# A hybrid encoder block on one core: the last pair's products ahead of the gate in front, the channel matrix in halves, a single-column first factor, and source order to the end

## The chip, the cores and the metric

The kernel runs on one core of one Trainium2 chip. A core has TensorE (matrix products into PSUM), VectorE, ScalarE and GpSimd (called PE, DVE, ACT and POOL in the profile) and SyncE (SP), whose queue issues most of the DMAs here. The metric is the device time of one execution in microseconds; lower is better.

## The reference

One layer of an encoder is applied to two sequences of 2048 tokens with 1024 features, with shared weights. Per sequence, all in float32:

```python
u = rmsnorm(h, g_norm)
q, k, v, ga, f, gf = split(u @ w_in)            # 512, 128, 128, 512, 512, 512 columns
q, k = rope(rmsnorm(q, g_q)), rope(rmsnorm(k, g_k))   # 8 q heads, 2 kv heads of 64; 2-D axial positions
a  = softmax(q k^T / 8) v * silu(ga)            # bidirectional
fo = (real(fft2(f over positions, 64 channels)) @ w_fmix per group) * silu(gf)
h  = h + concat(a, fo) @ w_out
h  = h + (p @ w_ple) * sigmoid(rmsnorm(h, g_ple) @ w_ple_gate)
y  = rmsnorm(h, g_final)
```

## The kernel before

Products that need float32 accuracy are made from float16 parts: an operand is split into a high part (`h`) and a low part (`l`), and a product is three matmuls, high by high, high by low and low by high (`SPLIT3`). A transposed operand is made by a transposing DMA. The kernel has two phases.

**Phase 1, `project`.** Tokens are taken in 16 pairs of 128-token tiles (8 pairs per sequence), in the loop `iteration(i)`, i up to 19, with `n` = 16. A pair passes through a software pipeline: load and normalise (`hi_u`, `lo_u`), q and kv products (`mm_tile(i, 0)` and `mm_tile(i, 1)`, in tiles `wr_q`, `wr_kv`), squares and Newton steps for q's and k's norms (`square_z`, `newton`, L669 to L687), norm and rotary position (`norm_q`, `rope_q`, with POOL's adds on L773), high and low parts (`hi_q` on ScalarE, L785; `lo_q` on VectorE, L797 to L801), and the transposes of q and k on SyncE's queue (L805, L808), whose results are stored one iteration later (L806, L810; in the last iteration by POOL's queue).

The remaining products of a pair are its sweep: a generator (`sweep_chunk`) that makes the f columns (8 steps), the gf columns (16), the first Fourier factor (1), and the gate ga (32 steps of three 256-column matmuls). Each `next` emits one step and returns its nominal time; `sweep_part(us)` takes steps up to a budget. So the budgets written in `iteration` decide where a pair's f, gf and gate products stand among the others. In iteration i the sweep is that of pair i-1. After a gate's matmuls, ScalarE takes the tanh (L1114), VectorE makes the SiLU from PSUM (L1117) and its maximum (L1095). Every fourth step also takes one step of `self.ahead`, which makes the maxima of the first attention units' scores (L1363, L1371) and then issues the transposition of the first unit's row maxima (`max_rows`, tile `mr`, L1387); every fifth takes one of `bg`, which prepares the far weights.

**Phase 2, attention with a filling.** `attention` runs 64 units (2 sequences, 2 kv heads, 16 query tiles) of 8 steps: scores (L1333, the first of them with `mr`), exponentials (ScalarE, L1336), row sums (POOL, L1341), maxima two units ahead (L1363, L1371), products with v (L1399). `interleave` fills the rest of TensorE with the generator `fill`: first `fourier2` (second factor of the position DFT, L1243, then the channel matrix `bd`, L1189, which is loaded from DRAM by L1220), then `outp`. `outp` handles 32 tiles of 128 tokens; for tile t it emits two slots `out1(t, 0..1)` (output projection and residual, L1586), then `out3(t-1, 0)`, `middle(t)`, `out3(t-1, 1)`. `middle(t)` takes squares (L1686), the norms by Newton steps (`norm`, L1692 to L1695), and makes the normalised and transposed `hT` that `out3(t, .)` needs one turn later (`out2`: L1715, L1716, L1719, L1721). `out3` ends with a tanh (L1599) and then the product with the embedding rows (`products`, on L505, sums on L1608 and L1610). A slot is 24 matmuls of 512 columns; before tile 30 the two halves of the rows of two neighbouring slots run side by side (`halves`, L1665, with the copy `seen` between), from tile 30 on (`WHOLE`) a slot is made whole (L505 in tiles `ps_x` or `ps_g`). VectorE's last operations of a slot are put off through `defer` and run at a `flush` while attention lasts (`self.dq` is a list), and at once when it has ended (`self.dq is None`).

The order on PE, ACT, DVE and SP is the order of the source in phase 1 (POOL as well) and during attention (`manual_schedule`). What is left when attention has ended is emitted by `self.drain(f)` in `run`, outside of that block, where a planner orders the instructions of all engines by its own costs. PSUM there: five banks `psD` (`ps_x`) besides the two of `psG` and one of `psF`.

Of the kernel before, what the change touches and what calls it, by code (L numbers as in the profile page):

```python
# [10 lines left out]
F32 = mybir.dt.float32  # L11
F16 = mybir.dt.float16
I32 = mybir.dt.int32
AF = mybir.ActivationFunctionType
ALU = mybir.AluOpType
# [4 lines left out]
DM = 1024  # L20
NT = 16
HD = 64
EPS = 1e-6
U_SC = 2.0 ** 8
# [21 lines left out]
_E = mybir.EngineType  # L46
# [119 lines left out]
class Build:  # L166
# [97 lines left out]
    def rsqrt(self, x, n, u="", e=None, st=None):  # L264

        st = st or self.st
        e = e or self.nc.vector
        tl = lambda m: st.tile([128, n], F32, name=f"rs{u}{n}_{m}", tag=f"rs{u}{n}_{m}", bufs=2)
        y, hx = tl("y"), tl("hx")
        e.tensor_scalar(out=y[:].bitcast(I32), in0=x.bitcast(I32), scalar1=-0.5, scalar2=float(0x5F3759DF),  # L270
                        op0=ALU.mult, op1=ALU.add)
        e.tensor_scalar(out=hx[:], in0=x, scalar1=-0.5, scalar2=None, op0=ALU.mult)
        for it in range(3):
            t, z = tl("t"), tl(f"z{it}")
            e.tensor_tensor(out=t[:], in0=y[:], in1=y[:], op=ALU.mult)
            e.tensor_tensor(out=t[:], in0=t[:], in1=hx[:], op=ALU.mult)
            c = 1.5 if it < 2 else 0.5
            w = z if it < 2 else tl("w")
            if e is self.nc.vector:
                e.scalar_tensor_tensor(out=w[:], in0=t[:], scalar=c, in1=y[:], op0=ALU.add, op1=ALU.mult)  # L280
            else:
                e.tensor_scalar(out=t[:], in0=t[:], scalar1=c, scalar2=None, op0=ALU.add)
                e.tensor_tensor(out=w[:], in0=t[:], in1=y[:], op=ALU.mult)
            if it == 2:
                e.tensor_tensor(out=z[:], in0=y[:], in1=w[:], op=ALU.add)
            y = z
        return y

    def pow2(self, name, m, exp):
# [331 lines left out]
    def project(self, P, PU, W, early, later, wkv, wq, wf, wgf, wga, bg, mid):  # L621
# [3 lines left out]
        nc, st = self.nc, self.st  # L625
# [183 lines left out]
                                        ks[:].rearrange("p v y t d -> p (v y t d)"))  # L809
            stores_next.append(lambda: self.last_stores.dma_start(self.kTd[s][:, :, c].rearrange("v p y r -> p v y r"), kT[:]))  # L810

        def sweep_part(us):

            while us > 0 and sweeps:
                try:
                    us -= next(sweeps[0])
                    if done:
                        done.append(True)
                        if len(done) % NBF == 0:
                            next(bg, None)  # L820
                        if len(done) % (NBF - 1) == 2:
                            next(self.ahead, None)
                except StopIteration:
                    del sweeps[0]
# [44 lines left out]
        def iteration(i):  # L869
# [11 lines left out]
                f()  # L881
            del stores[:]
            sq = square_z(i - 1) if ok(i - 1) else None
            if i == n + 1:
                sweep_part(3.9)
            if ok(i - 3):
                lo_q(i - 3)
            if ok(i - 2):
                rope_q(i - 2)
            rs = None  # L890
            if i == n:
                sweep_part(7.2)
            if ok(i - 1) or ok(i + 2):
                rs = newton(i - 1 if ok(i - 1) else None, i + 2 if ok(i + 2) else None, sq)
            if ok(i):
# [7 lines left out]
            if folds(i):  # L903
                fold_u(i, 0)
                fold_s(i, 0)
                fold_u(i, 1)
                sweep_part(12.0)
                fold_hl(i, 0)
                fold_s(i, 1)
            sweep_part(1000.0 if i < n else (3.3, 3.3, 7.0, 100.0)[i - n])  # L910
            if folds(i):
                fold_hl(i, 1)
            if ok(i + 2):
                hi_u(i + 2)
# [3 lines left out]
                load_x(i + 4, 1)  # L918
            if ok(i - 2):
                hi_q(i - 2)  # L920
            if ok(i):
                mm_tile(i, 1)
                append(i)
# [208 lines left out]
    def fourier2(self, pool, hook):  # L1132
# [84 lines left out]
            step()  # L1217
            yield 0.86

        nc.sync.dma_start(self.bd[:], self.bdd)  # L1220
        self.cx = pool.tile([128, 2, 128], F32, name="c2x", bufs=1)
        nc.sync.dma_start(self.cx[:], self.a["c_dft2x"].rearrange("v p c -> p v c"))
        for t in range(FP):
# [308 lines left out]
    def outp(self, pool0, ow, open_pool):  # L1532
# [87 lines left out]
        def slot(up, whole):  # L1620


            low = held.pop() if held else None
            def seen():
                j = st.tile([128, 1], F32, name="seen")
                nc.vector.tensor_copy(j[:], low[0][:, 0:1])  # L1626
# [9 lines left out]
            if up is not None:  # L1636
                ps = self.group_bank()
                for i, us in enumerate(self.mm(ps[:], up[0], up[1])):
                    yield us
                    yield from embed(i >= 6)  # L1640
                if low is not None:
                    seen()
                yield from self.after(ticket)
                yield from end(up[2](ps))
# [43 lines left out]
        def norm(ss, t):  # L1688

            ms = st.tile([128, 2], F32, name="h_ms")  # L1690
            e = nc.vector if self.dq is None or t == 0 or self.step >= 16 * N2 else nc.gpsimd
            e.tensor_scalar(out=ms[:], in0=ss[:], scalar1=1.0 / DM, scalar2=EPS, op0=ALU.mult, op1=ALU.add)  # L1692
            r = self.rsqrt(ms[:], 2, "h", e)
            q = st.tile([128, 1], F32, name="h_r")
            e.tensor_scalar(out=q[:], in0=r[:, 0:1], scalar1=U_SC, scalar2=None, op0=ALU.mult)  # L1695
            return q, r
# [68 lines left out]
        def middle(t):  # L1765

            q = r = None
            ss = st.tile([128, 2], F32, name="h_ss")
            if not (ok(t) and ok(t - 2)):
                nc.gpsimd.memset(ss[:], 1.0)  # L1770
            if ok(t - 2):
                yield from embed(True)
# [93 lines left out]
    def run(self):  # L1866
# [134 lines left out]
        self.step = 10 ** 9  # L2001
        att_stack.close()
        with pool("psD", 5, space=PSUM) as self.psX:
            self.drain(f)
        fill_stack.close()
        w_stack.close()

# [52 lines left out]
```

## Time and profile before

| | |
|---|---|
| median of 3 runs | 2585.57 us (2585.44 to 2585.97) |
| the profiled execution, own time | 2585.38 us |
| its span, first to last instruction | 2583.6 us |
| mean granted TensorE clock | 0.994 |
| TensorE busy in the span | 97% |
| phase 1 ends, first score of attention | 737.76 us |
| attention's last row sums | 2492.08 us |
| last matmul begins its group | 2572.43 us |

The first block of the page gives each engine's busy time and its share of the span. In a list of waits, a row says which instruction's group waited, for whom, how long in total, how often, and the longest. In a timeline, a row is a run of like instructions: start in us, length in us, engine, line, operation, out<-in, partitions x elements, count, and in brackets the idle time before it with what ended it. In a row of stretches, "DVE busy" and the like stand in the order PE, PEld, DVE, ACT, POOL, then the granted clock as a share of full speed. Times are from the start of the span.

### The profile page before, as it was taken

What the parts mean: (1) busy time and instruction counts of PE and PEld (TensorE: products, weight loads), DVE (VectorE), ACT (ScalarE), POOL (GpSimd) and SP (SyncE); (2) the same over time, 40 slices, a digit from 0 to 9 for tenths busy, and PEclk for the clock granted to TensorE, in tenths of its full rate; (3) what the DMA queues carried; (4) which work ended last, traced back from release to release, by engine and by line L of the source; (5) the groups of instructions that cost most, each with busy time, mean ns of one, the idle gap of its engine ahead of it and who ended that gap; (6) DMA issues with size and microseconds to landing.
All of it is one profiled execution on the core that took longest, in us unless ns stands there. A gap on an engine that the chain in (4) does not pass through costs nothing. (4 is left out here: it accounts for less than half of the span.)

```text
span 2583.6 us, 49739 instructions
## 1 busy us (share of the span) xinstructions
PE 2503.1 (97%) x19896; PEld 1381.7 (53%) x19896; DVE 1655.9 (64%) x2382; ACT 1185.5 (46%) x1983; POOL 1834.5 (71%) x1534
## 2 busy tenths in 40 slices
PE   6999999999989999999999999999999999999988
PEld 3566666666656554545555554445444554545533
DVE  7876675776566765676666666665666666666534
ACT  4443444443245545454544555445544444445532
POOL 0365453455469988888798888887887988888850
PEclk9999999999999999999999999999999999999999
DMA  8377687777287732232223233422233322322232
GB/s 260 90 202 198 187 245 209 184 195 192 62 254 226 211 90 64 56 80 73 70 56 80 60 92 77 97 66 72 64 80 79 71 74 60 71 78 77 78 76 53
DMA packets 459032, 297.91 MB, mean 115 GB/s; under 512 B 293840, under 2 KB 402128, under 8 KB 458800
## 3 DMA queue, kind: packets, MB, share of 16 engines
q1 hardware_dynamic: 437952, 256.28, 38.9%
q10 hardware_dynamic: 15712, 20.59, 2.4%
q0 software_dynamic: 5136, 17.87, 1.9%
q8 instruction: 155, 2.54, 0.4%
q14 instruction: 77, 0.63, 0.1%
HBM read 146.12 MB, written 82.45 MB: 88 GB/s over the span
## 5 line engine op out<-in xcount | busy, mean ns | idle before, releaser
L1341 POOL TENSOR_TENSOR acc<-acc,p 128x1024 f32<-128x1024 f32 x384 | 930.0, 2422 | 110.9 <-ACT p L1336 86.1
L1336 ACT ACTIVATE p<-ps_s,s_scale 128x512 f32<-128x512 f32 x1024 | 648.1, 684 | 638.2 <-PE ps_s L1333 621.9
L1371 DVE TENSOR_REDUCE a_mx<-ps_m 128x1 f32<-128x1024 f32 x498 | 608.8, 1223 | 512.7 <-PE ps_m L1363 501.5
L1665 PE MATMUL ps_g<-w_pg,hT 64*128 64x512 f16 x2784 | 494.7, 377 | 3.9 <-DVE seen L1626 2.4
L1399 PE MATMUL ps_o<-p,v 128*64 128x256 f32 x4096 | 468.1, 381 | 0.0
L1333 PE MATMUL ps_s<-q,k 64*128 64x512 f16 x3072 | 432.0, 377 | 1.4 <-ACT p L1336 1.0
L1399 PEld LDWEIGHTS ps_o<-p,v 128*64 128x64 f32 x4096 | 283.6, 137 | 159.9 <-issue 28.0
L505 PEld LDWEIGHTS <-uc 128*128 128x128 f16 x2400 | 236.1, 99 | 227.6 <-DMA uc<-hl 20.4
L1665 PEld LDWEIGHTS <-hT 64*128 64x128 f16 x2784 | 204.8, 94 | 156.6 <-issue 16.0
L1665 PE MATMUL ps_g<-w_wo,mh 64*128 64x512 f16 x1440 | 260.5, 376 | 3.8 <-DVE mh L1570 2.3
L1665 PE MATMUL ps_g<-w_wo,mT 64*128 64x512 f16 x1440 | 257.4, 376 | 0.6 <-DMA mT<-mh 0.6
L1333 PEld LDWEIGHTS <-k 64*128 64x128 f16 x3072 | 152.4, 94 | 194.9 <-issue 76.3
L1363 PE MATMUL ps_m<-k,q 64*128 64x512 f16 x996 | 200.7, 377 | 15.5 <-DVE a_mx L1371 15.3
L773 POOL TENSOR_TENSOR t<-t,t 128x640 f32<-128x640 f32 x32 | 49.3, 1560 | 205.2 <-DVE t L768 205.2
L505 PEld LDWEIGHTS <-w_ga 128*128 128x128 f16 x1536 | 148.8, 98 | 33.2 <-issue 10.4
L1339 POOL TENSOR_TENSOR acc<-p,p 128x1024 f32<-128x1024 f32 x64 | 151.0, 2359 | 13.0 <-ACT p L1336 12.2
L1665 PEld LDWEIGHTS <-mh 64*128 64x128 f16 x1440 | 101.6, 94 | 92.4 <-issue 16.8
L1665 PEld LDWEIGHTS <-mT 64*128 64x128 f16 x1440 | 107.1, 94 | 77.7 <-issue 4.8
L1422 DVE RECIPROCAL ps_f<-ps_f 128x256 f32<-128x256 f32 x61 | 107.1, 1756 | 13.6 <-PE ps_f L1415 13.6
L505 PE MATMUL ps_x<-uc,w_ga 128*128 128x256 f16 x1008 | 113.5, 273 | 0.6 <-DVE w_mxs L397 0.6
L840 POOL TENSOR_TENSOR f_s<-f_t 128x512 f32<-128x512 f32 x56 | 71.8, 1303 | 53.9 <-DVE uf L848 41.5
L1406 ACT ACTIVATE at<-ps_o,a_scale 128x256 f32<-128x256 f32 x64 | 30.4, 474 | 170.4 <-PE ps_o L1399 170.4
(343 smaller groups left out, 3363.6 us busy)
## 6 DMA issues: line engine op xcount, KB each, us to landing
q<-qTd SPq DMA_DIRECT2D x256, 64.0 KB, 2.2
ag<-agd SPq DMA_DIRECT2D x64, 256.0 KB, 3.5
out<-h POOLq DMA_DIRECT2D x31, 512.0 KB, 3.0
x<-in_x_prompt SPq DMA_DIRECT2D x16, 512.0 KB, 4.5
gfd<-gt ACTq DMA_DIRECT2D x32, 256.0 KB, 2.9
w_st<-in_w_out SPq DMA_DIRECT2D x32, 256.0 KB, 4.4
w_st<-in_w_ple_gate SPq DMA_DIRECT2D x32, 256.0 KB, 4.2
x<-in_x_sample SPq DMA_DIRECT2D x16, 512.0 KB, 5.8
```

Of the source, the lines that this page charges most:

```text
L505: self.nc.tensor.matmul(ps, lhs(ia, k), rhs(ib, k), start=(i == 0), stop=(i == 3 * ks - 1))
L773: nc.gpsimd.tensor_tensor(out=t1[:, tt], in0=t1[:, tt], in1=t2[:, tt], op=ALU.add)
L840: nc.gpsimd.tensor_tensor(out=FS[h][:, y], in0=x[:, 0], in1=x[:, 1], op=op)
L1333: nc.tensor.matmul(S[u][e][:], w[sl], q[sl].rearrange("p h q -> p (h q)"), start=j == i == 0, stop=i + 1 == len(todo), skip_group_check=True)
L1336: nc.scalar.activation(p[:, e, :], S[u][e][:], AF.Exp, scale=self.sc["s_scale"][:])
L1339: nc.gpsimd.tensor_tensor(out=ACC[u][:], in0=P[u, 0][:], in1=p[:], op=ALU.add)
L1341: nc.gpsimd.tensor_tensor(out=ACC[u][:], in0=ACC[u][:], in1=p[:], op=ALU.add)
L1363: nc.tensor.matmul(ps[c], Q[u][0][sl, h, :], kt[s, kv, half][sl, :, 0, :], start=True, stop=True)
L1371: nc.vector.reduce_max(MX[u][:, h, half, c:c + 1], x, axis=AX.X)
L1399: nc.tensor.matmul(o[64 * f:64 * f + 64], vt[s, kv, c // 8][:, c % 8, :], p[:, e, f], start=(c == 0), stop=(c == 15))
L1422: nc.vector.reciprocal(r, r)
L1665: nc.tensor.matmul(g[0][:], g[1](ia, k)[sl], g[2](ib, k)[sl], start=a, stop=z, skip_group_check=True)
```

## The change

- In the last iterations of `project` the budgets of `sweep_part` move. In iteration n-1 = 15 the rest of pair 14's gate steps is no longer swept before the second tile's q and kv products of pair 15, but in iteration 16 behind them, with `bare=True`, which takes no steps of `ahead` and `bg`. The two calls ahead of `lo_q` and ahead of `newton` go; `fold_hl(15, 1)` moves behind `hi_q(13)`. The later budgets are 13.2, 5.0 and the rest.
- `fourier2` loads the channel matrix `bd` with two DMAs, the half used first ahead of the other.
- `norm(ss, 0)`, of the first tile, uses a new `column_rsqrt`: one column, 10 instructions on VectorE with pointer scalars. The memset of `ss` on POOL is left out for tile 0.
- A whole slot in `outp` waits until attention has ended, and takes the embedding product from its fourth step on.
- The `drain` behind attention stands in a `manual_schedule` for PE, ACT, DVE and SP.

```diff
--- before.py
+++ after.py
@@ -284,6 +284,29 @@
             if it == 2:
                 e.tensor_tensor(out=z[:], in0=y[:], in1=w[:], op=ALU.add)
             y = z
+        return y
+
+    def column_rsqrt(self, ss):
+
+        st, v = self.st, self.nc.vector
+        n = 0
+
+        def op(x, a, b, o0, o1):
+            nonlocal n
+            n += 1
+            r = st.tile([128, 1], F32, name=f"cr{n}", tag=f"cr{n}", bufs=1)
+            v.tensor_scalar(out=r[:], in0=x, scalar1=a, scalar2=b, op0=o0, op1=o1)
+            return r[:]
+
+        x = op(ss, 1.0 / DM, EPS, ALU.mult, ALU.add)
+        y = st.tile([128, 1], F32, name="cr0", tag="cr0", bufs=1)[:]
+        v.tensor_scalar(out=y.bitcast(I32), in0=x.bitcast(I32), scalar1=-0.5, scalar2=float(0x5F3759DF),
+                        op0=ALU.mult, op1=ALU.add)
+        hx = op(x, -0.5, None, ALU.mult, ALU.bypass)
+        for it in range(3):
+            t = op(y, y, hx, ALU.mult, ALU.mult)
+            w = op(t, 1.5 if it < 2 else 0.5, y, ALU.add, ALU.mult)
+            y = w if it < 2 else op(w, y, U_SC, ALU.add, ALU.mult)
         return y
 
     def pow2(self, name, m, exp):
@@ -809,12 +832,12 @@
                                         ks[:].rearrange("p v y t d -> p (v y t d)"))
             stores_next.append(lambda: self.last_stores.dma_start(self.kTd[s][:, :, c].rearrange("v p y r -> p v y r"), kT[:]))
 
-        def sweep_part(us):
+        def sweep_part(us, bare=False):
 
             while us > 0 and sweeps:
                 try:
                     us -= next(sweeps[0])
-                    if done:
+                    if done and not bare:
                         done.append(True)
                         if len(done) % NBF == 0:
                             next(bg, None)
@@ -881,15 +904,11 @@
                 f()
             del stores[:]
             sq = square_z(i - 1) if ok(i - 1) else None
-            if i == n + 1:
-                sweep_part(3.9)
             if ok(i - 3):
                 lo_q(i - 3)
             if ok(i - 2):
                 rope_q(i - 2)
             rs = None
-            if i == n:
-                sweep_part(7.2)
             if ok(i - 1) or ok(i + 2):
                 rs = newton(i - 1 if ok(i - 1) else None, i + 2 if ok(i + 2) else None, sq)
             if ok(i):
@@ -904,11 +923,14 @@
                 fold_u(i, 0)
                 fold_s(i, 0)
                 fold_u(i, 1)
-                sweep_part(12.0)
+                sweep_part(12.0 if i < n - 1 else 8.6)
                 fold_hl(i, 0)
                 fold_s(i, 1)
-            sweep_part(1000.0 if i < n else (3.3, 3.3, 7.0, 100.0)[i - n])
-            if folds(i):
+            if i == n:
+                sweep_part(10.3, True)
+            elif i != n - 1:
+                sweep_part(1000.0 if i < n else (13.2, 5.0, 100.0)[i - n - 1])
+            if folds(i) and i < n - 1:
                 fold_hl(i, 1)
             if ok(i + 2):
                 hi_u(i + 2)
@@ -918,6 +940,8 @@
                 load_x(i + 4, 1)
             if ok(i - 2):
                 hi_q(i - 2)
+            if i == n - 1:
+                fold_hl(i, 1)
             if ok(i):
                 mm_tile(i, 1)
                 append(i)
@@ -1217,7 +1241,8 @@
             step()
             yield 0.86
 
-        nc.sync.dma_start(self.bd[:], self.bdd)
+        for v in (1, 0):
+            nc.sync.dma_start(self.bd[:, v], self.bdd[:, v])
         self.cx = pool.tile([128, 2, 128], F32, name="c2x", bufs=1)
         nc.sync.dma_start(self.cx[:], self.a["c_dft2x"].rearrange("v p c -> p v c"))
         for t in range(FP):
@@ -1621,6 +1646,9 @@
 
 
             low = held.pop() if held else None
+            while whole and self.dq is not None:
+                yield None
+
             def seen():
                 j = st.tile([128, 1], F32, name="seen")
                 nc.vector.tensor_copy(j[:], low[0][:, 0:1])
@@ -1637,7 +1665,8 @@
                 ps = self.group_bank()
                 for i, us in enumerate(self.mm(ps[:], up[0], up[1])):
                     yield us
-                    yield from embed(i >= 6)
+                    if i > 2:
+                        yield from embed(True)
                 if low is not None:
                     seen()
                 yield from self.after(ticket)
@@ -1688,7 +1717,9 @@
         def norm(ss, t):
 
             ms = st.tile([128, 2], F32, name="h_ms")
-            e = nc.vector if self.dq is None or t == 0 or self.step >= 16 * N2 else nc.gpsimd
+            if t == 0:
+                return self.column_rsqrt(ss[:, 0:1]), None
+            e = nc.vector if self.dq is None or self.step >= 16 * N2 else nc.gpsimd
             e.tensor_scalar(out=ms[:], in0=ss[:], scalar1=1.0 / DM, scalar2=EPS, op0=ALU.mult, op1=ALU.add)
             r = self.rsqrt(ms[:], 2, "h", e)
             q = st.tile([128, 1], F32, name="h_r")
@@ -1766,7 +1797,7 @@
 
             q = r = None
             ss = st.tile([128, 2], F32, name="h_ss")
-            if not (ok(t) and ok(t - 2)):
+            if t and not (ok(t) and ok(t - 2)):
                 nc.gpsimd.memset(ss[:], 1.0)
             if ok(t - 2):
                 yield from embed(True)
@@ -2001,7 +2032,8 @@
         self.step = 10 ** 9
         att_stack.close()
         with pool("psD", 5, space=PSUM) as self.psX:
-            self.drain(f)
+            with tc.manual_schedule(engines={_E.PE, _E.Activation, _E.DVE, _E.SP}):
+                self.drain(f)
         fill_stack.close()
         w_stack.close()
```

## The prediction

> **What bounds the kernel now.** I read the page first (busy shares, the chain that ended last), then TensorE's busy time and granted clock in stretches of 10 us, then what TensorE waited for in the stretches where it was not full, and last the order of instructions there.
>
> ```profile
> PE 2503.1 (97%) x19896; PEld 1381.7 (53%) x19896; DVE 1655.9 (64%) x2382; ACT 1185.5 (46%) x1983; POOL 1834.5 (71%) x1534
> ...
> 740.00:750.00 10.00, 3.02 (x24) 2.17 (x24) 5.99 (x11) 3.42 (x7) 3.21 (x6) 0.88 0.84 192
> 750.00:760.00 10.00, 8.77 (x48) 6.62 (x49) 3.60 (x4) 4.72 (x10) 5.46 (x7) 0.78 0.92 310
> ...
> 940.00:950.00 10.00, 6.66 (x44) 3.38 (x41) 6.47 (x6) 3.57 (x5) 9.58 (x6) 0.83 0.38 81
> ...
> PE ps_g L1189 <- DMA bd<-bdd: 5.8, 1, 5.8
> PE ps_g L1243 <- DVE gat L1117: 3.4, 1, 3.4
> ...
> PE ps_g L505 <- DVE h L1586: 4.2, 1, 4.2
> PE ps_g L1665 <- DVE seen L1626: 2.4, 1, 2.4
> ```
>
> TensorE is busy 97% of the span, so every edit counts only for the time in which TensorE stands still or runs slow. The second group of rows (length, then busy time of PE, PEld, DVE, ACT and POOL, granted clock, DMA share, GB/s) shows where: at 740 to 760, where the projections hand over to attention, and at 942 to 950, where the first tile is normalised for the gate. The last two groups are the waits of TensorE from 735 to 755 and from 2489 to 2575. The change touches just these three places.
>
> **The change part by part.** *First place: the handover at 738.* The rows are of TensorE, then VectorE and SyncE's queue, then POOL and ScalarE.
>
> ```profile
> 690.31 2.46 PE L505 MATMUL ps_x<-uc,w_ga 128*128 128x256 f16 x21
> 702.50 5.34 PE L505 MATMUL ps_g<-wr_q,uc 128*128 128x512 f16 x24
> 737.76 0.39 PE L1333 MATMUL ps_s<-mr,kone 64*128 64x512 f16 x2
> 742.39 0.94 PE L1243 MATMUL ps_g<-c,g_in 128*128 128x128 f32 x6 [3.37 <-DVE gat L1117]
> 751.23 2.05 PE L1189 MATMUL ps_g<-bd,fT 128*128 128x256 f32 x4 [5.82 <-DMA bd<-bdd]
> 753.07 1.06 PE L1243 MATMUL ps_f<-c,g_in 128*128 128x128 f32 x4
> 792.62 1.13 PE L1189 MATMUL ps_g<-bd,fT 128*128 128x256 f32 x4
> 793.59 0.61 PE L1243 MATMUL ps_f<-c,g_in 128*128 128x128 f32 x4
> ...
> 718.19 1.47 DVE L669 TENSOR_REDUCE q_ss<-sq 128x20 f32<-128x1280 f32 x1
> 723.44 0.22 DVE L687 TENSOR_SCALAR q_rs<-rsq_z,inv_kv 128x4 f32<-128x4 f32 x1
> 740.01 1.22 DVE L801 TENSOR_TENSOR qs<-t,qs 128x1024 f16<-128x1024 f32 x1
> 742.71 0.41 DVE L1117 SCALAR_TENSOR_TENSOR gat<-gat,ps_g 128x256 f32<-128x256 f32 x1
> ...
> 719.83 1.26 SPq L1387 DMA_TRANSPOSE mr<-nm  x1
> 741.29 2.61 SPq L805 DMA_TRANSPOSE qT<-qs  x2
> 744.00 2.00 SPq L808 DMA_TRANSPOSE kT<-ks  x1
> 746.06 0.97 SPq L1220 DMA_DIRECT2D bd<-bdd  x1
> ...
> mr<-nm SPq DMA_TRANSPOSE x1, 2.4
> ...
> 733.64 3.04 POOL L773 TENSOR_TENSOR t<-t,t 128x640 f32<-128x640 f32 x2 [3.96 <-DVE t L768]
> 736.71 1.06 ACT L785 ACTIVATE qs<-t 128x1024 f16<-128x1024 f32 x1 [6.22 <-POOL t L773]
> ```
>
> Both waits have one cause. The last pair's q and kv products (702.50) come after the whole gate of the pair in front (from 690.31). What follows them (square sums, Newton steps, rotary, split) reaches the low part of q only at 740.01. The last gate's SiLU (742.71) stands behind that on VectorE, and its PSUM bank is what the first Fourier product waits for: 3.4 us. On SyncE's queue the two q transposes and the k transpose (741.29, 744.00) stand ahead of the channel matrix's load (746.06), which lands at 751.2: 5.8 us.
>
> In the changed source, the sweep of the pair in front stops in iteration 15 after 8 steps of f, 16 of gf, the first factor and 5 of 32 steps of the gate; q and kv follow. So they start at 690.31 + 5 steps of 0.33 (a step is 3 matmuls; 21 took 2.46 with the last one's tail) = 692, not 702.5: 10.4 us earlier. The gate's other 27 steps go behind them; the sum of TensorE's work is the same. The chain, from the end of kv at 700: about 5 us for the older pairs' low parts and rotary on VectorE, 5.5 for the Newton steps (718.19 to 723.7), 3.4 for four gate SiLUs with their maxima, 0.41 each (742.71), that now queue behind them, 5 again for low part and rotary, 3.0 for POOL's adds (733.64), 1.9 for ScalarE (1.06 and two smaller copies), 2.8 for the low part: 727, not 741.2. VectorE is then free when the last gate leaves TensorE at 737.8, and the 3.4 us go.
>
> SyncE's queue: the transposes start at 727 to 729 (two buffers, whose stores must have landed) and take 2.6 + 2.0 us (741.29, 744.00). Behind them now stands the transposition of the first unit's maxima (mr, 719.83 before): the stretch marked bare takes no step of the maxima, so eight steps slip and mr is issued after the last pair's transposes. That is the added wait: issue at 732 to 734, landing 2.4 later (the row of transfers) or, with others in front, up to 3.5: 734 to 737.5, and the first score matmul (737.76) needs it. Late mr costs TensorE one for one; the cover is 0 to 3.5 us. The channel matrix's first half is issued right behind, at 733 to 735; the whole took 5.2 from issue to use, so the half is there by 740, and its first use falls at 742. The 5.8 us go. The second half costs one more issue on a queue that nobody waits for there; without that cover it is half of the 0.97 row. The bank of the postponed gates is held until VectorE comes to them, near 714; the products that take those banks next come at 712 to 720, so I book some loss.
>
> The clock: after the waits the same forms took 2.05 for 1.13 and 1.06 for 0.61 (751.23 and 753.07 against 792.62 and 793.59): with the next group about 1.6 us lost, which go too. The Trainium skill (TensorE: Matmul & The Clock Gate, Part 1: The HAM clock gate) has the clock halve after an idle window of about 3.4 us and stay so for a window; by it the price would be an estimated 1.7 us for each wait at 742 and 751, 3.4 in all. Against it, the dip at 940 to 950 (0.83) stands at a wait of 2.2 us, shorter than that window, so I take the rows.
>
> Bounds of this place: at best 3.4 + 5.8 + 1.6 = 10.8; at worst the 3.4 alone. For late mr and held banks I take 1.0 off: **9.8 gained**.
>
> *Second place: the first tile's factor.*
>
> ```profile
> 937.62 0.28 DVE L1692 TENSOR_SCALAR h_ms<-h_ss 128x2 f32<-128x2 f32 x1
> 940.10 0.15 DVE L1695 TENSOR_SCALAR h_r<-rsh_z 128x1 f32<-128x1 f32 x1
> 945.96 0.61 PE L1363 MATMUL ps_m<-k,q 64*128 64x512 f16 x2 [2.24 <-DVE a_mx L1371]
> ```
>
> 14 small instructions from 937.62 to 940.25, 0.19 each, become 10. The removed POOL memset stood in nobody's way. Two-column tensors become columns with operands by pointer, whose price no small row here shows; L687 with a pointer scalar took 0.22 (723.44), L1695 with a constant 0.15, so 7 of them may give back 0.5. Gain 0.3 to 0.8; TensorE's wait at 945.96 ends with this chain. **0.5.**
>
> *Third place: the end.* Two edits: the last two tiles' products wait until attention has ended (and so take the five new banks, not the two that the halves use), and four engines keep source order.
>
> ```profile
> 2495.76 0.39 PE L505 MATMUL ps_x<-w_wo,mh 128*128 128x512 f16 x1
> 2512.09 2.58 PE L505 MATMUL ps_g<-wp,pT 128*128 128x512 f16 x6 [4.18 <-DVE h L1586]
> 2547.82 5.34 PE L505 MATMUL ps_x<-w_pg,hT 128*128 128x512 f16 x24
> 2553.01 1.46 PE L505 MATMUL ps_g<-wp,pT 128*128 128x512 f16 x6
> 2554.30 5.34 PE L505 MATMUL ps_x<-w_pg,hT 128*128 128x512 f16 x24
> 2572.43 1.46 PE L505 MATMUL ps_g<-wp,pT 128*128 128x512 f16 x6
> ...
> 2548.81 1.06 ACT L1686 ACTIVATE h_hl<-h 128x1024 f16<-128x1024 f32 x1 [8.40 <-DVE h L1586]
> 2553.67 0.67 ACT L1599 ACTIVATE th<-ps_x,h_pg 128x512 f32<-128x512 f32 x1
> ...
> hT<-h_hl SPq DMA_TRANSPOSE x2, 6.3
> ...
> hT<-h_hl SPq DMA_TRANSPOSE x2, 4.6
> ```
>
> From 2495.76 TensorE has 10 slots of 24 matmuls (5.19 each, 2547.82 to 2553.01), 24 lone halves (streaming the same columns: 5.2) and 8 embedding products (1.29, 2553.01 to 2554.30): 67.4 us. It ends at 2573.9, 78.1 later. The 10.7 over are the waits 4.2 and 2.4 and 4.1 of slow clock behind them (six matmuls took 2.58 at 2512.09, 1.46 later). The wait of 4.2 is for the bank of an output slot that VectorE had not read; in the new banks it cannot arise. The `seen` copy now comes after 24 + 6 matmuls (6.5 us) that need nothing of it: the 2.4 go too.
>
> What is late next: the last tile's hT. In the trace the squares of h of tile 31 (2548.81) run ahead of the tanh of the slot in front (2553.67); in the source, `middle(31)` stands behind that slot and its tanh. So from that slot's end: tanh 0.7, two squares 2.2, the small steps 2.6 (as from 937.62), high and low part of hT's source 2.5, the second transposition's landing 4.6 (the last row: the pair issued from 2553.8) = 12.6 us. TensorE has 1.29 + 5.19 + 1.29 = 7.8 to cover it: a new wait of 4.8 us, plus 1.4 of slow clock (between the 1.1 of the row at 2512.09 and the 1.6 above). The rest of the source order I followed for SyncE (store of the last attention tile, loads, transposes) and VectorE: all have several us of cover; the load of tile 31's x now stands behind tile 30's transposes and lands some 2 us after its slot's sums, with nothing waiting. After the last matmul the same 9.7 us remain. **10.7 - 4.8 - 1.4 = 4.5 gained**; bounds 2.8 (a landing of 6.3, as the pair from 2530 took) and 10.7.
>
> **Sum.** 9.8 + 0.5 + 4.5 = 14.8 us. The profiled execution took 2585.38 (span 2583.6 and 1.8 around it): 2570.6. The median shown, 2585.57, lies 0.2 above it: **2570.8**.
>
> **The rivals.** (a) The squares still come early, and no wait opens at the last hT: 6.2 better, 2564.6. For it: the chain has its data at 2548.8. Against: ScalarE is to keep source order. (b) The handover keeps a wait of 4 to 6 us, because mr comes behind the last pair's transposes or the first half still lands late: 2575 to 2577. For it: mr's thin cover; DMA share 0.84 there. (c) Slower: in source order VectorE's sums of each embedding product queue behind the Newton chain, and with two banks for those products each of the six last gate slots waits for a bank. Newton 2.6 and two squares 2.2 make at most 4.8 a slot, 28.8 in all, against 10.3 from the first two places and 10.7 of waits that went: 2585.6 - 21.0 + 28.8 = 2593.4. It decides from 26.2 us, 4.4 a slot. Against: only one slot of each pair has that chain ahead of it. (d) The change does little: mr late by its whole transposition chain (some 8 us) and the wait at the end twice as long: 2570.8 + 8 + 5 = 2583.8.
>
> **How the numbers follow.** Forecast 0.63, (a) 0.14, (b) 0.15, (c) 0.03, (d) 0.05. The forecast's own range is 2567 to 2574; with (a) and (b) 2563 to 2578. Faster 0.92, same 0.05, slower 0.03; 0.2% (5.2 us) is about what a measurement of this kernel can tell from no change.
>
> **What would show it.** Right: no wait of TensorE at L1243 or L1189 before attention's first products, q's last transposes issued before 731, clock near 1.0 where 0.88 and 0.78 stood; no wait for `seen` or h in the tail, one wait of about 5 us for hT at the last tile's first gate slot. Wrong: a wait for mr at the first scores; TensorE waiting for gate SiLUs between 700 and 720; no wait at the last hT.

## The result, and the profile after

The changed kernel takes 2568.45 us (median of 4 runs, 2566.73 to 2570.77) against 2585.51 (4 runs, 2584.95 to 2585.97): ratio 0.9935, 95% interval 0.9917 to 0.9952, 17.1 us less. The forecast was 2570.8. The profiled execution of after took 2568.06, span 2566.3. Measured again later, beside the last experiments (`after_again`), the same kernel took 2574.04 against 2586.85 (0.9950, interval 0.9937 to 0.9963): 12.8 us less. Single executions differ by several us, so below two kernels are compared by spans inside their profiles, and medians only where the interval allows it.

The line numbers in the rows of after are those of the kernel after (each kernel of an experiment has its own): L505 became L528, L1333 L1358, L1363 L1388, L1371 L1396, L1243 L1268, L1189 L1213, L1719 L1750. The page's first block, and the stretches (length, busy time of PE, PEld, DVE, ACT, POOL, granted clock, DMA share, GB/s) that answer to those of before:

```profile
PE 2498.8 (97%) x19896; PEld 1379.8 (54%) x19896; DVE 1653.9 (64%) x2378; ACT 1184.6 (46%) x1983; POOL 1836.8 (72%) x1533
...
720.00:730.00 10.00, 5.96 (x18) 2.05 (x16) 8.26 (x20) 2.36 (x4) 3.75 (x3) 0.66 0.69 180
...
740.00:750.00 10.00, 10.00 (x84) 7.71 (x82) 4.74 (x9) 5.27 (x10) 2.37 (x7) 1.00 1.00 339
750.00:760.00 10.00, 10.00 (x79) 6.46 (x79) 6.98 (x10) 5.92 (x12) 8.95 (x5) 1.00 0.80 276
...
940.00:950.00 10.00, 10.00 (x93) 6.07 (x94) 4.97 (x6) 4.27 (x9) 7.80 (x6) 1.00 0.24 60
```

740 to 760 is now full at full clock (3.02 and 8.77 busy before), and so is 940 to 950. But 720 to 730 has become a hole: 5.96 busy at a clock of 0.66. What TensorE waited for there and at the end (list of waits of after, two rows), and the timeline of TensorE, VectorE and SyncE's queue:

```profile
PE ps_x L528 <- DVE a_mx L1396: 4.0, 1, 4.0
...
PE ps_x L528 <- DMA hT<-h_hl: 2.7, 2, 2.1
...
691.95 5.34 PE L528 MATMUL ps_x<-wr_q,uc 128*128 128x512 f16 x24
714.26 3.40 PE L528 MATMUL ps_x<-w_gf,uc 128*128 128x512 f16 x15
724.07 5.76 PE L528 MATMUL ps_x<-w_gf,uc 128*128 128x512 f16 x15 [4.04 <-DVE a_mx L1396]
744.33 0.39 PE L1358 MATMUL ps_s<-mr,kone 64*128 64x512 f16 x2
745.51 0.94 PE L1268 MATMUL ps_g<-c,g_in 128*128 128x128 f32 x6
748.47 1.13 PE L1213 MATMUL ps_g<-bd,fT 128*128 128x256 f32 x4
...
715.22 0.42 DVE L1119 TENSOR_REDUCE tmax<-gat 128x1 f32<-128x256 f32 x1
718.73 0.42 DVE L820 TENSOR_TENSOR kd<-kd,ks 128x256 f32<-128x256 f32 x1 [3.10 <-ACT ks L810]
721.46 1.96 DVE L791 TENSOR_TENSOR t<-qn,rt 128x256 f32<-128x256 f32 x8
723.34 1.28 DVE L1396 TENSOR_REDUCE a_mx<-ps_x 128x1 f32<-128x512 f32 x2
729.64 1.22 DVE L824 TENSOR_TENSOR qs<-t,qs 128x1024 f16<-128x1024 f32 x1
...
735.58 1.26 SPq L1412 DMA_TRANSPOSE mr<-nm  x1
738.89 0.94 SPq L1245 DMA_DIRECT2D bd<-bdd  x2
```

The waits at L1268 and L1213 are gone. A new one of 4.0 us stands at 724, in the gf products of the last sweep: their PSUM bank still holds scores of the first units, whose maxima VectorE reduces at 723.34, behind the low parts of pair 14 (from 718.73) and the rotary position (721.46). 15 matmuls behind it took 5.76 for 3.40. So attention's first score comes at 744.33, 6.6 later than before.

The first products of the row sums of each attention unit (L1415 before, L1440 after) align the kernels. Gain over the profiled execution of before, in us:

| kernel | unit 2 | unit 5 | unit 7 | unit 53 | unit 63 | last row sums to the end of the span |
|---|---|---|---|---|---|---|
| before (at) | 847.50 | 929.40 | 984.72 | 2225.01 | 2492.08 | 91.5 |
| after | 5.1 | 5.4 | 7.8 | 11.2 | 10.6 | 84.8 |
| front_only | 4.7 | 5.0 | 4.5 | 7.8 | 7.8 | 90.9 |
| bd_only | 0.1 | 0.2 | -0.7 | 3.5 | 3.5 | 96.0 |
| tail_only | 0.6 | 1.0 | 3.9 | 4.9 | 4.9 | 84.2 |
| column_only | 0.0 | 0.3 | 1.5 | 5.0 | 5.0 | 91.8 |
| planner_drain | 5.5 | 4.3 | 3.0 | 5.3 | 5.3 | 87.8 |
| early_squares | 3.3 | 3.7 | 6.7 | 8.5 | 8.5 | 81.7 |
| maxima_first | 8.4 | 7.2 | 6.2 | 7.6 | 7.6 | 85.8 |
| low_behind | 3.7 | 2.4 | 5.5 | 6.6 | 6.6 | 87.8 |
| after_again | 1.1 | 1.3 | 0.0 | 3.8 | 3.8 | 84.8 |
| all_three | 8.7 | 9.0 | 11.9 | 15.6 | 15.6 | 81.5 |
| bd_whole | 6.0 | 6.4 | 6.4 | 9.4 | 9.4 | 85.4 |

Column unit 2 is the handover, 5 to 7 the first tile, the last column the end. Each row is one execution, and executions of the same code differ: at the handover the kernels that share after's `project` (after, front_only, planner_drain, early_squares, low_behind, after_again, bd_whole) read 1.1 to 6.0. Part of that was lost or gained before any edit, since their last pair's first q product, ahead of which they are alike, begins anywhere from 690.37 (bd_whole) to 694.37 (early_squares). From that product to unit 2 they take 149.2 to 152.0 us. The unchanged end takes 90.9 to 96.0 (before, front_only, bd_only, column_only), after's end 84.2 to 87.8 (six profiles). A difference of 3 us in one column of two single profiles is therefore no proof by itself; it counts where the traces show the wait that makes it.

### The profile page after: what moved, and what is told of

Read it like the earlier page. It is cut to its first block, busy times and chain, and to the rows that moved or that the text cites. A ratio compares the mean times of both kernels' runs of the same rounds, so it can differ in the third digit from the quotient of the medians.

```text
span 2566.3 us, 49731 instructions
## 1 busy us (share of the span) xinstructions
PE 2498.8 (97%) x19896; PEld 1379.8 (54%) x19896; DVE 1653.9 (64%) x2378; ACT 1184.6 (46%) x1983; POOL 1836.8 (72%) x1533
## 5 line engine op out<-in xcount | busy, mean ns | idle before, releaser
L1396 DVE TENSOR_REDUCE a_mx<-ps_m 128x1 f32<-128x1024 f32 x498 | 608.7, 1222 | 512.0 <-PE ps_m L1388 500.6
L1358 PE MATMUL ps_s<-q,k 64*128 64x512 f16 x3072 | 432.0, 377 | 1.4 <-ACT p L1361 1.0
L528 PEld LDWEIGHTS <-uc 128*128 128x128 f16 x2400 | 235.8, 99 | 232.4 <-DMA uc<-hl 19.7
L1358 PEld LDWEIGHTS <-k 64*128 64x128 f16 x3072 | 152.4, 94 | 195.0 <-issue 76.3
L1388 PE MATMUL ps_m<-k,q 64*128 64x512 f16 x996 | 200.5, 376 | 13.0 <-DVE a_mx L1396 13.0
L528 PEld LDWEIGHTS <-w_ga 128*128 128x128 f16 x1536 | 149.8, 98 | 33.8 <-issue 9.5
L1694 PEld LDWEIGHTS <-mh 64*128 64x128 f16 x1440 | 101.7, 94 | 90.9 <-issue 16.6
L528 PE MATMUL ps_x<-w_gf,uc 128*128 128x512 f16 x480 | 108.6, 385 | 4.0 <-DVE a_mx L1396 4.0
L528 PE MATMUL ps_x<-uc,w_ga 128*128 128x256 f16 x960 | 109.8, 275 | 0.2 <-DVE w_mxs L420 0.2
```

What stands on the lines that cost most here:

```text
L528: self.nc.tensor.matmul(ps, lhs(ia, k), rhs(ib, k), start=(i == 0), stop=(i == 3 * ks - 1))
L1358: nc.tensor.matmul(S[u][e][:], w[sl], q[sl].rearrange("p h q -> p (h q)"), start=j == i == 0, stop=i + 1 == len(todo), skip_group_check=True)
L1388: nc.tensor.matmul(ps[c], Q[u][0][sl, h, :], kt[s, kv, half][sl, :, 0, :], start=True, stop=True)
L1396: nc.vector.reduce_max(MX[u][:, h, half, c:c + 1], x, axis=AX.X)
L1694: nc.tensor.matmul(g[0][:], g[1](ia, k)[sl], g[2](ib, k)[sl], start=a, stop=z, skip_group_check=True)
```

## The experiments

**The parts one by one.** Each is the kernel before with some of the change's edits: `front_only` those of `project`, `bd_only` the two DMAs of `bd`, `column_only` `column_rsqrt`, `tail_only` the two edits of the end; `bd_whole` is the changed kernel with `bd` in one DMA:

```diff
-        for v in (1, 0):
-            nc.sync.dma_start(self.bd[:, v], self.bdd[:, v])
+        nc.sync.dma_start(self.bd[:], self.bdd)
```

> The kernel before with the edits of `project` alone (q and kv of pair 15 ahead of pair 14's gate); channel matrix in one DMA, old factor, old end. Theory A (from the trace of after: the wait of 4.0 us for the maxima's bank and some 2.4 us of slow clock eat more than half of the handover's 10.8): 4.3 to 5.4 us faster than before, 2580 to 2581, first score at about 744.3. Theory B (the prediction's step as written, 9.8 us): 2576, first score at 738. Theory C (the early queue is worth little without the halves of the channel matrix): the wait at the first channel product stays at 3 us or more and the gain is under 2 us.

2579.19 us, ratio 0.9971 (0.9959 to 0.9982): 4.7 to 10.6 us less, which alone leaves both A and B open. The profile shows theory A: the new wait is there without the other parts (rows of front_only), no wait is left at the Fourier and channel products, and 4.7 us are gained at unit 2. That span speaks against theory B (9.8), and the missing wait at the first channel product against C.

```profile
725.21 5.00 PE L505 MATMUL ps_x<-w_gf,uc 128*128 128x512 f16 x15 [3.57 <-DVE a_mx L1372]
748.84 1.13 PE L1190 MATMUL ps_g<-bd,fT 128*128 128x256 f32 x4
```

> The kernel before with the channel matrix loaded in halves and nothing else. Its load still stands behind the last transposes (issue at 746). Theory A (landing time goes with bytes): the wait of 5.8 us falls by about half of the 5.2 us between issue and use, 2.6 us, 2583. Theory B (landing is mostly a fixed delay, or the other transfers set it): at most 0.5 us, 2585.0 to 2585.6.

2586.44, ratio 0.9998 (0.9989 to 1.0008): nothing that can be measured, theory B. The wait did fall from 5.82 to 3.62, but that is not the halves' doing in the main. The products behind the wait in front (3.36, as before) ran slow here, 1.65 for 0.94, so TensorE came to the wait later. From the load's issue to its first use it took 4.50 us (746.40 to 750.90), against 5.17 in before; with the whole matrix it took 4.75 in column_only and 5.14 in tail_only, with waits of 3.8 and 4.4.

```profile
742.74 1.65 PE L1244 MATMUL ps_g<-c,g_in 128*128 128x128 f32 x6 [3.36 <-DVE gat L1117]
750.90 2.04 PE L1189 MATMUL ps_g<-bd,fT 128*128 128x256 f32 x4 [3.62 <-DMA bd<-bdd]
```

> The changed kernel with the channel matrix in one DMA. Theory A (once SyncE's queue is early the load has time to spare: issued at 738.9 and first used at 748.5, against the 5.2 us that it took before): no change, 2567.5 to 2569.5. Theory B (the halves carry part of the gain): a wait at the first channel product of 1 us or more, 2569.5 or slower.

2568.91, ratio to before 0.9926 (0.9912 to 0.9939): theory A. The whole matrix was issued at 736.90 and its first product ran at 746.58 without a wait. With the early queue the halves bring nothing.

> The kernel before with the first tile's single-column factor alone. Theory A (the trace of after, exponentials aligned across the first tile: 5.4 us ahead in front of it, 7.7 behind it): 1.5 to 2.3 us faster, 2583.2 to 2584. Theory B (the prediction's term): 0.5 us, 2585.0. Theory C (the extra at the first tile comes from the handover's shift and not from the factor): within 0.3 us of before.

2582.49, ratio 0.9992 (0.9982 to 1.0003), so the runs decide nothing. By the table 1.2 us come between units 5 and 7, near A; but the chain itself is only some 0.3 shorter (below), and `tail_only`, with the old factor and the old handover, gained 2.9 there. None of the three theories is right: the gain at the first tile has another source.

> The kernel before with the two edits of the end alone (last slots wait until attention has ended; source order kept in the drain). Theory A (the trace of after, aligned on attention's last exponentials): 6.7 us faster, 2578.8, with a wait of about 2.7 us for hT of the last tile. Theory B (the prediction's term): 4.5 us, 2581, with 4.8 us of wait. Theory C: the end gained only because it started at another phase; alone it gains under 3 us.

2576.48, ratio 0.9971 (0.9960 to 0.9981). From the last row sums to the end 84.2 us against 91.5, 7.3 less: theory A, with the same waits for hT (2.09 and 0.62).

**The new wait at the handover.** `maxima_first` moves one pair of VectorE instructions of the changed kernel:

```diff
+            if i == n + 1:
+                sweep_part(6.5)
             if ok(i - 3):
                 lo_q(i - 3)
...
-                sweep_part(1000.0 if i < n else (13.2, 5.0, 100.0)[i - n - 1])
+                sweep_part(1000.0 if i < n else (5.7, 5.0, 100.0)[i - n - 1])
```

> The changed kernel with one pair of VectorE instructions moved: in iteration 17 the first 6.5 us of the sweep stand ahead of `lo_q`, so that the two reductions of the first unit's maxima (ahead of the low part of q and the rotary position instead of behind them) free their PSUM bank early; the order on the other engines is the same. Theory A (that bank is the cause of the wait at 724): the wait of 4.0 us and the slow clock behind it go, first score at 738 to 739, 5 to 6.4 us faster than the changed kernel: 2562 to 2564. Theory B (the bank of a gate whose SiLU stands at 724.5 would be waited for next): 2 to 4 us of wait stay, 2565 to 2568. Theory C (mr's landing at 738, which had 6 us to spare, becomes the end of phase 1): a wait for mr at the first score of 1 to 3 us, 2564 to 2566.

```profile
715.18 1.28 DVE L1398 TENSOR_REDUCE a_mx<-ps_x 128x1 f32<-128x512 f32 x2
...
717.55 5.35 PE L528 MATMUL ps_x<-w_gf,uc 128*128 128x512 f16 x24
730.34 0.39 PE L1390 MATMUL ps_x<-k,q 64*128 64x512 f16 x2 [2.85 <-DVE gt L1143]
740.37 0.39 PE L1360 MATMUL ps_s<-mr,kone 64*128 64x512 f16 x2
```

The reduction stands at 715.18, the wait of 4.0 is gone and the 24 gf matmuls run through: the bank of the maxima was the cause. Theory B is right in kind about what comes next: the bank of the second gf product, whose SiLU (L1143) stands behind the last pair's low part, 2.85, without slow clock. The first score comes at 740.37, and at unit 2 the kernel is 3.4 us ahead of after. No wait for mr, so not C. The edit moves just that pair of reductions: the order on TensorE, POOL and SyncE is the same as in after. But the whole took 2569.35 (0.9939, 0.9926 to 0.9951), no better than the changed kernel: by the table it is 1.6 behind after at unit 7 and 2.9 at unit 63.

**Where they went: the first tile.** Rows of VectorE, POOL and TensorE around 940, first of before, then of maxima_first, of tail_only and of early_squares:

```profile
941.52 3.25 DVE L1719 SCALAR_TENSOR_TENSOR h_hl<-h,h_r,h_hl 128x1024 f16<-128x1024 f32 x1 [1.28 <-ACT h_hl L1715]
941.35 5.63 POOL L1341 TENSOR_TENSOR acc<-acc,p 128x1024 f32<-128x1024 f32 x2
946.50 4.88 PE L1399 MATMUL ps_o<-p,v 128*64 128x256 f32 x32
```

```profile
933.99 3.21 DVE L1752 SCALAR_TENSOR_TENSOR h_hl<-h,cr,h_hl 128x1024 f16<-128x1024 f32 x1 [1.28 <-ACT h_hl L1748]
933.78 5.63 POOL L1368 TENSOR_TENSOR acc<-acc,p 128x1024 f32<-128x1024 f32 x2
938.39 0.61 PE L1390 MATMUL ps_m<-k,q 64*128 64x512 f16 x2 [2.21 <-DVE a_mx L1398]
938.93 6.23 PE L1426 MATMUL ps_o<-p,v 128*64 128x256 f32 x32
```

```profile
940.55 1.28 DVE L1723 SCALAR_TENSOR_TENSOR h_hl<-h,h_r,h_hl 128x1024 f16<-128x1024 f32 x1 [1.28 <-ACT h_hl L1719]
940.63 5.85 POOL L1341 TENSOR_TENSOR acc<-acc,p 128x1024 f32<-128x1024 f32 x2
943.02 0.39 PE L1363 MATMUL ps_m<-k,q 64*128 64x512 f16 x2 [0.28 <-DVE a_mx L1371]
```

```profile
937.53 1.47 DVE L1750 SCALAR_TENSOR_TENSOR h_hl<-h,cr,h_hl 128x1024 f16<-128x1024 f32 x1 [1.28 <-ACT h_hl L1746]
937.87 5.79 POOL L1366 TENSOR_TENSOR acc<-acc,p 128x1024 f32<-128x1024 f32 x2
940.18 0.39 PE L1388 MATMUL ps_m<-k,q 64*128 64x512 f16 x2 [0.46 <-DVE a_mx L1396]
```

The low part of the first tile's h takes 1.28 where VectorE begins 0.08 us ahead of POOL's addition of the row sums, and 3.2 where POOL is 0.2 ahead: then it ends 1.08 us after the first of POOL's two additions, as if it had waited for it. It does so in all eight profiles in which POOL was first or both began within 0.03 us. Where VectorE is first, POOL's first addition takes 3.4 (tail_only) instead of 2.34. The reduction of maxima behind it, and with it TensorE, is that much later; and after a wait of 2.2 us 32 matmuls took 6.23 for 3.67. The Trainium skill (SBUF — State Buffer, Who interferes with whom) has an instruction of VectorE with two SBUF inputs and one of GpSimd that reads SBUF exclude each other, whichever issues first holding the port to its end; the rows agree. front_only shows the same on a tiny instruction of the old factor, which takes 0.16 elsewhere in that chain and here ends with POOL's addition:

```profile
934.95 2.34 POOL L1342 TENSOR_TENSOR acc<-acc,p 128x1024 f32<-128x1024 f32 x1
935.04 2.27 DVE L280 SCALAR_TENSOR_TENSOR rsh_z<-rsh_t,rsh_z 128x2 f32<-128x2 f32 x1
```

In that profile ScalarE's exponentials then stood behind the late factor, and TensorE waited 3.96 us for them. The new factor's pointer instructions have a single tensor as input; in after and column_only its last ones ran beside an operation of POOL at their usual 0.21.

`low_behind` takes the reduction out from behind that instruction:

```diff
             if t:
                 return self.defer_slow(fin)
-            fin()
-            return [self.nflush]
+
+            def fin0():
+                fin()
+                tk[0] = [self.nflush - 1]
+
+            due.append((self.nflush + 1, fin0))
...
-                if ok(t):
+                if t == 0:
+                    out2(t, q)
+                elif ok(t):
                     tk[t] = out2(t, q)
```

> The changed kernel with one VectorE instruction moved: the low part of the first tile's h stands behind the next reduction of maxima and not ahead of it; the order on the other engines is the same. In the profiles so far that low part took 1.28 to 1.47 us where it began before POOL's addition of the row sums (two profiles) and 2.3 to 3.4 where POOL had begun first (seven), and the reduction behind it released TensorE that much later. Theory A (the two instructions exclude each other, and the race between them sets TensorE's wait of 0.5 to 2.4 us at the first tile, after which its clock is halved in some executions): the wait falls below 0.6 us in any order and the clock stays at 1.00, first tile as in the fastest profile: 1.2 us faster than the profile of the changed kernel, up to 4.8 faster than executions with a slow clock there; median 2565 to 2567. Theory B (hT's low part then lands too late for the first gate slot): a wait for hT of 1 to 2 us near 943, 2568 or slower. Theory C: no difference, 2568 to 2569.

> The changed kernel itself, for its spread on the chip of the two kernels beside it. If the race at the first tile makes its spread, its executions fall between 2565 and 2572 as before, wider than those of the kernel in which the race is taken away (low part behind the maxima). If the spread has other sources, both are equally wide.

```profile
938.85 1.34 DVE L1750 SCALAR_TENSOR_TENSOR h_hl<-h,cr,h_hl 128x1024 f16<-128x1024 f32 x1
939.08 5.78 POOL L1366 TENSOR_TENSOR acc<-acc,p 128x1024 f32<-128x1024 f32 x2
941.19 3.67 PE L1424 MATMUL ps_o<-p,v 128*64 128x256 f32 x32
```

low_behind has no wait for the maxima there, none for hT, and full clock; from unit 5 to 7 it gained 3.1 on before's execution, where after_again on the same chip, with a wait of 2.45, lost 1.2. That fits theory A, but doesn't prove the move's worth: VectorE happened to begin first here too (by 0.23 us), and in tail_only and early_squares, where it did so in the old order, the wait was only 0.28 and 0.46 and the gain 2.9 and 3.0. What the move saves when POOL is first, no profile shows. The median did not show it either: 2570.66 against 2574.04, intervals 0.9920 to 0.9949 and 0.9937 to 0.9963, which overlap. And the part on the spread was wrong: low_behind's executions lie between 2562 and 2575, after_again's between 2572 and 2575. The race is not what makes the spread, or not alone; what does stays open.

**The end.**

```diff
+            if t == N2 - 1:
+                yield from middle(t)
             if ok(t - 1):
                 yield from wait(tk, t - 1)
                 yield from along(slot(out3(t - 1, 0), t >= WHOLE), pr)
-            if t:
+            if t and t != N2 - 1:
                 yield from middle(t)
```

> The changed kernel with `middle(31)` ahead of the gate slot out3(30, 0) and not behind it: on ScalarE the squares of tile 31 stand ahead of that slot's tanh, on VectorE the Newton steps ahead of its two sums; TensorE's and SyncE's orders are the same. Theory A (the last hT is late because its squares stand behind the tanh): hT lands by 2539, the waits of 2.10 and 0.63 us at the last gate slot go, 2.7 to 3 us faster than the changed kernel: 2565.5. Theory B (another wait takes its place, for the bank of an embedding product or for h of tile 30): no faster than 2567.5.

> The changed kernel without the source order in the drain: the planner orders ScalarE, VectorE and SyncE behind attention (TensorE's order is the same). Theory A (rival (a) of the prediction: the planner put the squares early, so the wait for the last hT goes): 2.7 us faster than the changed kernel, 2565.8. Theory B (the planner's order brings other waits of before back): slower than the changed kernel by 2 to 4 us, 2570 to 2572. Theory C: the slots' wait alone made the gain and source order changes nothing, within 0.5 us.

early_squares: 81.7 us from the last row sums to the end, 84.8 in after: 3.1 less, no wait for hT; theory A. In runs 2563.09, ratio 0.9906 (0.9891 to 0.9921), an interval that still overlaps that of the changed kernel. planner_drain: 87.8, 3.0 more; 2573.35, 0.9946 (0.9934 to 0.9959). Its one long wait behind attention is again that of an embedding product for its bank (rows: timeline of planner_drain), and none is for hT. In before that bank was held by an output slot (L1586); here it is held by the embedding product before it, whose sum (L1635) the planner put behind another instruction that waited 9.25 us for ScalarE. So theory B; the squares are early under the planner, as A said, but that is paid elsewhere. The medians of early_squares and planner_drain lie clearly apart, those of either and the changed kernel do not.

```profile
2506.58 2.72 PE L528 MATMUL ps_g<-wp,pT 128*128 128x512 f16 x6 [4.19 <-DVE h L1635]
```

Of the 6.7 us at the end the edit of the slots alone gives 3.7 and source order 3.0, by one profile each. The waits roughly account for the 3.0 (4.2 and some 2 of slow clock against 2.7), but low_behind, with after's order, took 87.8 as well, through a slow clock behind its wait for hT.

**All three moves together.** The move of `maxima_first` has 6.7 in place of 5.7 here, which also puts the SiLU of the second gf product ahead of the last low part.

> The changed kernel with three moves of order and no other edit: the maxima's reductions and the second gate's SiLU of iteration 17 ahead on VectorE and ScalarE (budgets 6.5 and 6.7), `middle(31)` ahead of its gate slot, and the first tile's low part behind the next maxima. If the terms add up: handover 5 to 6.4 us, less up to 1 for a later mr; end 3.0; first tile 1.2 to 2: 9 to 11 us faster than the changed kernel, 2558 to 2560. If the handover's gain is given back at the first tile for another cause than the race of VectorE and POOL: 2563 to 2565.

2564.04 (2559.80 to 2566.96), ratio 0.9912 (0.9901 to 0.9924); after_again on the same chip 2574.04 with an interval that lies wholly above: 10 us less, which is what the terms were expected to add up to, though the level, on a chip where the changed kernel is slower too, is 2564 and not 2558 to 2560. In the profile the 3.6 us on after at unit 2 (0.2 of them there before the moves) and the 3.3 at the end go with the waits that their moves shorten or remove. At the first tile VectorE was again first, by 0.43 us, so what that move contributes is not shown. It beats both kernels. What TensorE still waits for from 700 to 760:

```profile
PE ps_x L1390 <- DVE a_mx L1398: 1.0, 1, 1.0
PE ps_x L1390 <- DVE gt L1143: 0.4, 1, 0.4
PE ps_s L1360 <- DMA mr<-nm: 0.4, 1, 0.4
```

mr's transposition, with 5.3 us to spare in after (landed at 738.98), is now late by 0.4: the next bound of this place.

## Why the prediction was right, point by point

**The handover, 9.8 forecast, 5.1 measured.** The mechanism held: q and kv at 691.95 (forecast 692), both waits and the slow clock behind them gone, channel matrix issued at 738.89, ten us ahead of its use. The last pair's q transposes were issued at 730.92 (forecast 727 to 729, and before 731 as a sign of being right). mr was issued at 735.58 (forecast 732 to 734) and landed at 738.98, later than the forecast's latest, 737.5; nothing waited for it only because the first score had slipped to 744.33. At the 737.76 of before it would have been late by 1.2, so on that term the forecast was lucky. The step that failed is the sentence on held banks, booked with mr at 1.0 us. It looked at the postponed gates, whose SiLUs stood at 712 to 715.6 as forecast and held no product of TensorE, and not at the maxima, whose reduction stands behind the low part and the rotary position of that iteration in VectorE's order and came at 723.3. Price 4.0 us and 2.4 of slow clock, against 1.0. Why the low part of pair 14 began only at 718.73 (VectorE waited 3.10 us for ScalarE's copy, and ScalarE had itself waited 9.22 us for one of the postponed SiLUs) was read from the trace and not tried. Rival (b), a wait of 4 to 6 us at the handover, came true here in size, by another cause than the two that it named, and not in its total.

**The first tile, 0.5 forecast.** The factor as such was near its lower end. The 10 instructions took 2.33 us (rows of after, first to last), 14 before 2.63; seven operations with pointers cost 0.27 each, above the 0.22 of the nearest row.

```profile
932.18 0.14 DVE L298 TENSOR_SCALAR cr<-h_ss 128x1 f32<-128x1 f32 x1
...
932.62 1.89 DVE L298 TENSOR_SCALAR cr<-cr,cr 128x1 f32<-128x1 f32 x7
...
935.78 2.61 DVE L1750 SCALAR_TENSOR_TENSOR h_hl<-h,cr,h_hl 128x1024 f16<-128x1024 f32 x1 [1.28 <-ACT h_hl L1746]
939.57 0.39 PE L1388 MATMUL ps_m<-k,q 64*128 64x512 f16 x2 [1.60 <-DVE a_mx L1396]
939.89 3.67 PE L1424 MATMUL ps_o<-p,v 128*64 128x256 f32 x32
```

Of the 2.4 us of the table (units 5 to 7) 1.9 are the wait of 1.60 for 2.24 and the full clock behind it, 3.67 for 4.88. The wait hangs on the race of VectorE and POOL, which the prediction did not see although its two rows stood in the trace of before, and what the clock then costs varies (last section). So the 2.4 are mostly luck of one execution and not the change's: between the same units after_again, the same kernel, lost 1.2 and bd_whole gained nothing.

**The end, 4.5 forecast, 6.7 measured.** The two waits of before (4.2 and 2.4) and the slow clock behind them went, and one for hT came, at the place named: 2.7 us, not 4.8.

```profile
2542.06 0.61 PE L528 MATMUL ps_x<-w_pg,hT 128*128 128x512 f16 x2 [2.10 <-DMA hT<-h_hl]
2543.29 4.92 PE L528 MATMUL ps_x<-w_pg,hT 128*128 128x512 f16 x22 [0.63 <-DMA hT<-h_hl]
...
2540.13 1.29 SPq L1752 DMA_TRANSPOSE hT<-h_hl  x1
```

The mis-sized term is the chain of 12.6 us: it took 11.1 (2532.2 to 2543.3), since the second transposition landed 3.1 after its issue, not 4.6, and the first two matmuls began on the high part alone. The 1.4 of slow clock was 0 in this execution and 3.0 in low_behind, whose same 22 matmuls behind the same wait took 7.88. That is 3.5 better than booked, and 1.3 of it is missing in the 6.7: some 0.7 of the 10.7 was neither wait nor slow clock and stayed (TensorE's 70.8 us without the 2.7 of waits are 68.1, not 67.4), and the time after the last matmul was 10.3 where 9.7 was booked (it varies between these two values from profile to profile). Rival (a) needed the squares early: early_squares shows its mechanism, worth 3.1 in that profile and not 6.2.

**What no step named.** Between units 7 and 53 after gained 3.4 us on the profiled execution of before. Every kernel gained there, from 1.0 (tail_only) over 3.3 (front_only), 3.5 (column_only) and 3.7 (after_again) to 4.2 in bd_only, which is before but for one load that was over by then. So that execution of before was slow there, for a reason that stays open, and I don't count the 3.4 as the change's. Without them the gain of the spans is 17.3 - 3.4 = 13.9, forecast 14.8. The total was right because an overrated handover (-4.7) stood against an underrated end (+2.2) and first tile (+1.9). That the errors cancelled is luck, and the 1.9 is luck of one execution; the two measurements of the medians, 17.1 and 12.8 us, lie on either side of the forecast.

Rivals (c) and (d) did not occur: no slot of the end waits for a bank, and mr had 5.3 us to spare.

## What to carry to other kernels

When products are moved earlier, list for each PSUM bank in the rotation who empties it and what stands ahead of that instruction on its engine: here a reduction that nobody had waited for became the longest wait, and moving it ahead of the low part and the rotary position gave 3.4 of the 6.4 us back. Gains in one stage can be eaten by a race in the next; align two traces at the same instruction and follow the gain along the kernel before believing a term. A change of a few us is judged by such spans and by the waits in them, over more than one profile: stages of this kernel whose code is the same differ by up to 5 us between executions.

## What the runs showed of the hardware

Two instructions, one on VectorE with two SBUF operands and one on POOL, exclude each other: the low part took 1.28 to 1.55 us where VectorE was first by 0.08 to 0.43 (four profiles), 1.28 where it ran between two additions (front_only), and 2.3 to 3.5 where POOL was first, or both began within 0.03 us (eight).

The clock's price of a wait isn't set by its length. The wait of 2.1 and 0.6 us for the last hT cost nothing in after, tail_only and after_again (22 matmuls in 4.92), 1.0 and 1.1 in maxima_first and bd_whole (5.89 and 6.02, the second wait 0.35), and 3.0 in low_behind (7.88, a row of its timeline, at a mean granted clock of 0.62):

```profile
2546.03 0.60 PE L528 MATMUL ps_x<-w_pg,hT 128*128 128x512 f16 x2 [2.07 <-DMA hT<-h_hl]
2547.38 7.88 PE L528 MATMUL ps_x<-w_pg,hT 128*128 128x512 f16 x22 [0.74 <-DMA hT<-h_hl]
```

At the first tile a wait of 1.60 cost none, one of 1.30 cost 1.3 (column_only, 4.96 for 3.67), and those of 2.1 to 2.45 cost 1.2 to 2.6 (6.23 for 3.67 in maxima_first, at a clock of 0.58); shorter waits, of 0.6 to 0.9 and of 0.2 us, stood just ahead of each. The Trainium skill (TensorE: Matmul & The Clock Gate, Part 1: The HAM clock gate) has an activity window that runs freely and is not reset when a kernel starts. That would give such differences between executions, but no run here shows the window itself. That the clock falls after an idle window of about 3.4 us does not agree with these rows, where it fell behind waits of 1.3 to 2.45 us.
